# Two kinds of rows: operand pairs and plain rows that begin 32 bytes behind a multiple of 2048, beside rows that begin on one

## The chip, the core and the metric

The kernel runs on one core of a Trainium2 chip. The metric is the device time of one execution in microseconds (us); a smaller number is better. All times below come from runs of this kernel and from one execution that the hardware profiler recorded.

## The reference

Two layers of a block with four parallel branches work on a sequence of 512 tokens (the "x stream") and on a context of 256 tokens (the "context stream"), with a width of 1024. Per layer and stream:

```python
hx = modulate(rmsnorm(x, norm_w[l]), shift_x, scale_x)      # the same for the context
px = split_proj(hx @ w_in[l])                               # 1024 -> 11008 columns
r = head_group_norm(retention(px)) * silu(ret_z)            # branch 0
s = sc_b * conv3(sc_c * sc_x) * silu(sc_z)                  # branch 1
f = silu(layer_norm(conv31(a * sigmoid(g)))) * silu(cf_z)   # branch 2
a = windowed_gqa(px, context keys and values) * silu(att_z) # branch 3
merged = sum(sigmoid(gate_i) * (branch_i @ w_branch[i]))
x = x + gate_x * (merged @ w_out[l])
```

The context stream is computed in full in the first layer; in the second one only its keys and values are needed. The result is rmsnorm(x) * final_norm_w. Everything is float32.

## The kernel before

**Work.** Activations lie with the 1024 features on the 128 partitions, in 8 chunks, and with the tokens along the row. A product of full accuracy is made from three products of a fast format (fp32r): each operand is split into a high part (`hi`, made by ScalarE, ACT) and a low part (`lo`, what is left, made by VectorE, DVE), and TensorE (PE) adds hi·hi, hi·lo and lo·hi over the chunks:

```python
for j, (a, b) in enumerate(((hi, xh), (hi, xl), (lo, xh))):
    nc.tensor.matmul(ps, a[:, cs(i)], b.r[:, o:o + t], ...)
```

Here `a` is the weight block (stationary, 128 columns) and `b` the activation row (moving, `t` columns): 512 columns in the x stream, 256 in the context stream. These are the products with the outputs `d` in the profile. Each of them loads its own weights. Transposes and small products in plain float32 write the outputs `k` and `ov`.

**Stages in order of time.** Start (modulation vectors from the weights `w_m`, norm of the context, first projections): to about 50 us. Context stream of layer 0: to about 392 us. x stream of layer 0: to about 1090 us. Keys and values of the context in layer 1: to about 1120 us. x stream of layer 1 and the final norm: to the end.

**Rows.** Activations, split parts and many loaded weights live in 59 rows of 2048 bytes for each partition (128 x 512 float32 or fp32r) and 12 half rows. `Arena.get` hands out the row at the head of one list of free rows; a row comes back to the tail of the list when the Python object dies, which is when the last instruction that uses it has been recorded. What is handed out next to the same row has to wait on the chip until the last reader of the old content is done. `row()` gives a plain row, `part()` a row for one split part, and `pair()` for 256 columns gives one row for both parts (`r51h` in the first 1024 bytes, `r51l` behind it). A tile `fill` of 480 float32 stands ahead of the rows; in the built program it puts the first row at byte 18432 of a partition, which is 9 times 2048, so every row begins on a multiple of 2048 and every low half of a pair 1024 bytes behind one. The split weights `wh`, `wl` begin on multiples of 2048 as well.

**Order.** PE runs in the order in which the code issues its work. The other engines and the DMA queue of SyncE (SP), through which all loads go, run in an order that a scheduler chooses from the dependences, those through reused rows among them. In the start, `start()` loads per step four rows of `w_m` (`mod_load`), splits them (`mod_pe`) and multiplies them; in the first three steps it also splits a weight block that was loaded in two rows (`w_load`, `w_split`, output `wl`). The context stream loads its weights into rows too, the x stream mostly into two tiles of their own.

Of the kernel before, what the change touches and what calls it, by code (L numbers as in the profile page):

```python
# [8 lines left out]
F32 = mybir.dt.float32  # L9
# [16 lines left out]
P = 128  # L26
# [90 lines left out]
    return c  # L117


NROWS = 59  # L120
PAD = 480


class Row:
# [3 lines left out]
    def __init__(self, free, ring, tile, w, parts):  # L128
        self.free, self.ring = free, ring
        self.r = tile[:, :w] if parts else None  # L130
        self.a = tile[:, :w].bitcast(F32) if parts else tile[:, :w]
# [20 lines left out]
        self.ring = None  # L152


class Arena:


    def __init__(self, pool, n, nh):
        self.full = [pool.ring(2048, name=f"row{i}") for i in range(n)]
        self.half = [pool.ring(1024, name=f"hrow{i}") for i in range(nh)]  # L160
        self.n = 0

    def get(self, w, parts, keep, pair=False):
        free = self.half if keep and w <= 256 else self.full
        if not free:
            self.relief(free)
        ring = free.pop(0)
        self.n += 1
        if pair:
            both = Both(free, ring)  # L170
            return [Half(both, ring.tile([P, 256], F32R, name=f"r{self.n}{x}"), w, True) for x in "hl"]
        t = ring.tile([P, 256 if free is self.half else 512], F32R if parts else F32, name=f"r{self.n}")
        return Row(free, ring, t, w, parts)
# [104 lines left out]
class Block:  # L278
    def __init__(self, ctx, tc, xc, vec, cst, w_a, w_g, w_b, w_o, w_m, out):
        self.tc, self.nc = tc, Tally(tc.nc)  # L280
        self.xc, self.out = xc, out
        self.wsrc = {"a": w_a, "g": w_g, "b": w_b, "o": w_o}
        self.w_m = w_m

        rp = ctx.enter_context(tc.tile_pool(name="rp", bufs=1))
        rp.tile([P, PAD], F32, name="fill")
        self.arena = Arena(rp, NROWS, 12)
        self.arena.relief = self.relief

        self.cp = cp = ctx.enter_context(tc.tile_pool(name="cp", bufs=1))  # L290
        self.wraw = [cp.tile([P, 1024], F32, name=f"w{i}") for i in range(2)]
        self.wt = [[cp.tile([P, 1024], F32R, name=f"w{p}{i}") for p in "hl"] for i in range(3)]
        self.pt = [cp.tile([P, 640], F32, name=f"p{i}") for i in range(6)]
        pp = ctx.enter_context(tc.tile_pool(name="pp", bufs=1, space=PSUM))
        nc = self.nc
        self.cst = cp.tile([P, NC_], F32, name="cst")
        self.vec = cp.tile([P, NV], F32, name="vec")
        nc.sync.dma_start(self.vec, vec)
        nc.sync.dma_start(self.cst[:, :NCE], cst[:, :NCE])
        self.late_consts = lambda: nc.sync.dma_start(self.cst[:, NCE:], cst[:, NCE:])  # L300
        self.rings = {}
        self.dense = [pp.tile([P, 512], F32, name=f"d{i}") for i in range(3)]
        self.ovs = [pp.tile([P, 512], F32, name="ov")]
        self.work = [pp.tile([P, 512], F32, name=f"k{i}") for i in range(4)]
        self.turn = {}
        self.wq, self.wraws, self.wready, self.wkeep = [], [], {}, {}
        self.lanes = [[] for _ in range(5)]
        self.turns = 0
        self.flow = None
# [1161 lines left out]
```

## Time and profile before

| | |
|---|---|
| median of 3 runs | 1832.25 us (1831.04 to 1833.5) |
| the profiled execution | 1832.62 us, of which its span is 1830.5 us |
| PE busy | 1799.5 us, 98% of the span |
| weight loads (PEld) busy | 1562.1 us, 85% |
| DVE busy | 1329.4 us, 73% |
| ACT busy | 847.1 us, 46% |
| mean granted TensorE clock | 0.994 |

A matmul's busy time in the profile covers its way through the array, so that of neighbouring products overlaps (283 ns for one with 256 columns); what counts is the distance from the start of one to the start of the next, called spacing below. It is read from a row with starts, or as a count of products in a stretch.

### The profile page before, as it was taken

What the parts mean: (1) busy time and instruction counts of PE and PEld (TensorE: products, weight loads), DVE (VectorE), ACT (ScalarE), POOL (GpSimd) and SP (SyncE); (2) the same over time, 40 slices, a digit from 0 to 9 for tenths busy, and PEclk for the clock granted to TensorE, in tenths of its full rate; (3) what the DMA queues carried; (4) which work ended last, traced back from release to release, by engine and by line L of the source; (5) the groups of instructions that cost most, each with busy time, mean ns of one, the idle gap of its engine ahead of it and who ended that gap; (6) DMA issues with size and microseconds to landing.
All of it is one profiled execution on the core that took longest, in us unless ns stands there. A gap on an engine that the chain in (4) does not pass through costs nothing. (4 is left out here: it accounts for less than half of the span.)

```text
span 1830.5 us, 27546 instructions
## 1 busy us (share of the span) xinstructions
PE 1799.5 (98%) x10224; PEld 1562.1 (85%) x10224; DVE 1329.4 (73%) x2643; ACT 847.1 (46%) x1616; POOL 27.9 (2%) x34
## 2 busy tenths in 40 slices
PE   6999999999999999999999999999999999999997
PEld 4999999998888888788888889888888888888887
DVE  8899999884556669996898457447999865444445
ACT  6666765553554544423423336445534554323232
POOL 1000000000000000000000000000000000000000
PEclk8999999999999999999999999999999999999999
DMA  8736377743122222233555552322122222332233
GB/s 306 252 125 213 111 242 231 235 138 116 69 70 67 84 81 83 91 108 124 185 170 168 169 182 75 116 70 70 66 91 87 80 98 87 115 104 87 87 117 114
DMA packets 104646, 232.60 MB, mean 127 GB/s; under 512 B 12864, under 2 KB 20800, under 8 KB 104512
## 3 DMA queue, kind: packets, MB, share of 16 engines
q1 hardware_dynamic: 104512, 230.84, 37.9%
q8 instruction: 80, 1.31, 0.3%
q14 instruction: 54, 0.44, 0.1%
HBM read 218.73 MB, written 5.24 MB: 122 GB/s over the span
## 5 line engine op out<-in xcount | busy, mean ns | idle before, releaser
L187 PE MATMUL d<-r,wh 128*128 128x512 f32 (+1 forms) x3136 | 942.7, 383 | 0.3 <-DVE r L187 0.3
L187 PEld LDWEIGHTS d<-r,wh 128*128 128x128 f32 x3136 | 572.7, 188 | 106.2 <-DVE r L187 0.5
L187 PE MATMUL d<-r,wl 128*128 128x512 f32 (+1 forms) x1568 | 597.6, 381 | 0.0
L187 DVE TENSOR_TENSOR wl<-w,wh 128x1024 fp32r<-128x1024 f32 x193 | 235.6, 1221 | 233.8 <-ACT wh L187 229.0
L187 ACT ACTIVATE wh<-w 128x1024 fp32r<-128x1024 f32 x193 | 205.0, 1062 | 411.5 <-PE d L187 358.2
L187 PEld LDWEIGHTS d<-r,wl 128*128 128x128 f32 x1568 | 294.8, 188 | 57.6
L187 ACT ACTIVATE r<-r 128x512 fp32r<-128x512 f32 (+3 forms) x264 | 150.5, 588 | 211.6 <-DVE r L187 94.5
L187 DVE TENSOR_TENSOR r<-r,r 128x512 fp32r<-128x512 f32 (+5 forms) x338 | 207.8, 629 | 35.2 <-ACT r L187 31.2
L187 DVE SCALAR_TENSOR_TENSOR r<-r,h_cfw,r 128x503 f32<-128x503 f32 (+19 forms) x360 | 229.1, 648 | 2.0
L187 PE MATMUL d<-r,r 128*128 128x512 f32 x768 | 184.8, 389 | 0.5 <-DVE r L187 0.5
L187 ACT ACTIVATE wh<-r 128x512 fp32r<-128x512 f32 x208 | 129.2, 631 | 101.7 <-PE d L187 88.5
L187 PEld LDWEIGHTS d<-r,r 128*128 128x128 f32 x768 | 144.1, 188 | 30.8 <-DVE r L187 0.9
L187 DVE TENSOR_TENSOR wl<-r,wh 128x512 fp32r<-128x512 f32 x208 | 140.6, 685 | 18.6 <-ACT wh L187 17.5
L187 DVE SCALAR_TENSOR_TENSOR r<-r,d 128x512 f32<-128x512 f32 (+1 forms) x156 | 92.7, 594 | 56.4 <-PE d L187 32.4
L187 ACT ACTIVATE r<-d 128x512 f32<-128x512 f32 (+2 forms) x234 | 118.5, 507 | 14.1 <-PE d L187 9.5
L187 PE MATMUL k<-r,r 128*128 128x128 f32 (+2 forms) x752 | 112.3, 290 | 2.7 <-ACT p L187 2.6
L187 ACT ACTIVATE r<-k 128x512 fp32r<-128x512 f32 (+4 forms) x162 | 76.9, 522 | 70.5 <-PE k L187 69.2
L187 PEld LDWEIGHTS k<-r,r 128*128 128x128 f32 x752 | 99.5, 191 | 8.9 <-ACT p L187 6.2
L187 ACT ACTIVATE p<-k,s_nm 128x256 f32<-128x256 f32 (+1 forms) x144 | 69.7, 497 | 78.0 <-DVE s_nm L187 77.9
L187 DVE SCALAR_TENSOR_TENSOR r<-r,cs,r 128x256 f32<-128x256 f32 x196 | 83.6, 477 | 2.0 <-DMA r<-w_m 1.4
L187 DVE TENSOR_TENSOR r<-k,r 128x512 fp32r<-128x512 f32 (+2 forms) x88 | 54.4, 651 | 9.5 <-ACT r L187 9.3
L187 ACT ACTIVATE p<-p,s_rc 128x512 f32<-128x512 f32 (+2 forms) x80 | 51.3, 719 | 9.6 <-DVE s_rc L187 9.6
(393 smaller groups left out, 2245.3 us busy)
## 6 DMA issues: line engine op xcount, KB each, us to landing
w<-w_a SPq DMA_DIRECT2D x108, 512.0 KB, 3.5
r<-w_a SPq DMA_DIRECT2D x128, 256.0 KB, 5.0
w<-w_g SPq DMA_DIRECT2D x64, 512.0 KB, 3.5
r<-w_m SPq DMA_DIRECT2D x96, 256.0 KB, 3.8
r<-w_b SPq DMA_DIRECT2D x96, 256.0 KB, 3.4
r<-w_g SPq DMA_DIRECT2D x64, 256.0 KB, 3.8
w<-w_o SPq DMA_DIRECT2D x21, 512.0 KB, 3.5
r<-xc SPq DMA_DIRECT2D x24, 256.0 KB, 3.8
```

Source lines behind the costliest of these rows:

```text
L187: return f(*a, **k)
```

## The change

The rows now come in two lists. `full` holds 36 rows, which begin on multiples of 2048 as before; `odd` holds 24 rows in a pool of their own, behind a tile of 32 bytes, so they begin 32 bytes behind a multiple of 2048. A further tile of 504 float32 brings what follows (the split weights among it) back to a multiple of 2048. `Arena.get` looks through the lists in an order that depends on the use: a row for one split part of more than 256 columns comes from `full` if it has a free row, otherwise from `odd`; a plain row, and a pair for 256 columns, comes from `odd` if it has a free row, otherwise from `full`. In all there are 60 rows in place of 59.

```diff
-NROWS = 59
+NROWS = 36
+NODD = 24
 PAD = 480
@@
+class Kinds:
+    def __init__(self, lists):
+        self.lists = lists
+
+    def __bool__(self):
+        return any(self.lists)
+
+    def first(self):
+        return next(x for x in self.lists if x)
@@
-    def __init__(self, pool, n, nh):
+    def __init__(self, pool, n, odd, nodd, nh):
         self.full = [pool.ring(2048, name=f"row{i}") for i in range(n)]
         self.half = [pool.ring(1024, name=f"hrow{i}") for i in range(nh)]
+        self.odd = [odd.ring(2048, name=f"orow{i}") for i in range(nodd)]
@@
     def get(self, w, parts, keep, pair=False):
-        free = self.half if keep and w <= 256 else self.full
-        if not free:
-            self.relief(free)
+        if keep and w <= 256:
+            kinds = Kinds([self.half])
+        elif parts and not pair:
+            kinds = Kinds([self.full, self.odd])
+        else:
+            kinds = Kinds([self.odd, self.full])
+        if not kinds:
+            self.relief(kinds)
+        free = kinds.first()
         ring = free.pop(0)
@@
         rp = ctx.enter_context(tc.tile_pool(name="rp", bufs=1))
         rp.tile([P, PAD], F32, name="fill")
-        self.arena = Arena(rp, NROWS, 12)
+        ro = ctx.enter_context(tc.tile_pool(name="ro", bufs=1))
+        ro.tile([P, 8], F32, name="fill1")
+        self.arena = Arena(rp, NROWS, ro, NODD, 12)
+        rf = ctx.enter_context(tc.tile_pool(name="rf", bufs=1))
+        rf.tile([P, 504], F32, name="fill2")
```

In the built programs, 2688 of the 3488 products with 256 moving columns and 128 weight columns have their moving row 32 bytes behind a multiple of 64 after the change (of the 5248 with 512 columns, 136); before, it is none of either.

PE issues the same products in the same order up to about 850 us; from there on some transposes of the convolution branch stand a few products later. The other queues change from the start on. On SP in the start, before (`r52` to `r55` and `r68` to `r71` are rows of `w_m` for two steps, `r56` and `r57` the two halves of a weight block; in brackets the semaphores that the load waits for, DVE and PE for readers of the row's old content, DMAHW for earlier loads):

```order
L187 DMA r52_349<-w_m 128x512 [waits DMAHW2_49]
L187 DMA r53_350<-w_m 128x512 [waits DMAHW3_49]
L187 DMA r54_351<-w_m 128x512 [waits DMAHW4_49]
L187 DMA r55_352<-w_m 128x512 [waits DMAHW5_49]
L187 DMA r56_357<-w_a 128x512 [waits DMAHW6_49]
L187 DMA r57_358<-w_a 128x512 [waits DMAHW7_49]
L187 DMA r68_410<-w_m 128x512 [waits DMAHW0_49,DVE_49]
L187 DMA r69_411<-w_m 128x512 [waits DMAHW1_49,PE_49]
L187 DMA r70_412<-w_m 128x512 [waits DMAHW2_49,PE_49]
L187 DMA r71_413<-w_m 128x512 [waits DMAHW3_49,PE_49]
```

The same loads after the change:

```order
L210 DMA r52_358<-w_m 128x512
L210 DMA r53_359<-w_m 128x512 [waits DMAHW3_49]
L210 DMA r56_366<-w_a 128x512 [waits DMAHW4_49]
L210 DMA r57_367<-w_a 128x512 [waits DMAHW5_49]
L210 DMA r54_360<-w_m 128x512 [waits DMAHW6_49,DMAHW0_49,DVE_49]
L210 DMA r55_361<-w_m 128x512 [waits DMAHW7_49,DMAHW1_49,DVE_49]
L210 DMA r68_419<-w_m 128x512 [waits PE_49]
L210 DMA r69_420<-w_m 128x512 [waits DVE_49]
L210 DMA r70_421<-w_m 128x512 [waits DMAHW4_49,DMAHW2_49,DVE_49]
L210 DMA r71_422<-w_m 128x512 [waits DMAHW5_49,DMAHW3_49,DVE_49]
```

`r54` and `r55` now wait for DVE and stand behind `r56` and `r57`: they lie where `r39` and `r40` (the halves of the third weight block) lay, and `r70` and `r71` where `r56` and `r57` lie. Later in the start, `r110` lies where `r94` lay. On DVE at the same step, before (`wl2` is the low half of a weight block, a `TENSOR_TENSOR` with two rows the low part of a row of `w_m`):

```order
L187 TENSOR_TENSOR r75_427<-r53_350,r74_426 128x512
L187 SCALAR_TENSOR_TENSOR r66_404<-r6_183,mod0_164,r49_338 128x256
L187 TENSOR_TENSOR r77_435<-r54_351,r76_434 128x512
L187 TENSOR_TENSOR r79_443<-r55_352,r78_442 128x512
L187 TENSOR_TENSOR wl2_142<-r56_357,wh2_141 128x512
L187 TENSOR_TENSOR wl2_142<-r57_358,wh2_141 128x512
```

And after the change:

```order
L210 TENSOR_TENSOR r75_436<-r53_359,r74_435 128x512
L210 TENSOR_TENSOR wl2_151<-r56_366,wh2_150 128x512
L210 TENSOR_TENSOR wl2_151<-r57_367,wh2_150 128x512
L210 SCALAR_TENSOR_TENSOR r66_413<-r6_192,mod0_173,r49_347 128x256
L210 TENSOR_TENSOR r77_444<-r54_360,r76_443 128x512
L210 TENSOR_TENSOR r79_452<-r55_361,r78_451 128x512
```

The split of the weight block moved ahead of that of `r54` and `r55`.

## Rows read from the trace of the kernel before

**Rows 1.** The page's part 1: busy us (share) x instructions

```profile
PE 1799.5 (98%) x10224; PEld 1562.1 (85%) x10224; DVE 1329.4 (73%) x2643; ACT 847.1 (46%) x1616; POOL 27.9 (2%) x34
```

**Rows 2.** The page's part 2: tenths busy in 40 slices of 46 us

```profile
PE   6999999999999999999999999999999999999997
...
DVE  8899999884556669996898457447999865444445
...
PEclk8999999999999999999999999999999999999999
```

**Rows 3.** PE's waits in the whole span: us in total, times, longest

```profile
PE k L187 <- DVE r L187: 8.0, 6, 2.2
PE k L187 <- DVE s L187: 7.0, 1, 7.0
PE k L187 <- ACT p L187: 4.2, 12, 0.7
```

**Rows 4.** Busy time by windows, the start and the context stream: PE, PEld, DVE, ACT, POOL

```profile
0.00:52.00 52.00, 37.05 (x229) 25.14 (x229) 42.58 (x142) 33.66 (x70) 4.85 (x7) 0.87 0.91 318
...
60.00:368.00 308.00, 308.00 (x2572) 307.25 (x2571) 284.71 (x680) 188.34 (x416) 6.37 (x7) 1.00 0.60 196
```

**Rows 5.** Windows in the context stream, products with 256 columns alone

```profile
255.00:285.00 30.00, 30.00 (x252) 30.00 (x252) 28.02 (x64) 17.77 (x37) 0.00 (x0) 1.00 0.83 263
...
270.00:282.00 12.00, 12.00 (x102) 12.00 (x102) 10.50 (x23) 7.31 (x16) 0.00 (x0) 1.00 0.77 235
```

**Rows 6.** Windows in the x stream, products with 512 columns alone

```profile
1600.00:1768.00 168.00, 168.00 (x743) 139.12 (x742) 73.45 (x93) 49.41 (x70) 0.00 (x0) 1.00 0.29 99
1600.00:1612.00 12.00, 12.00 (x55) 9.93 (x54) 5.37 (x7) 3.44 (x5) 0.00 (x0) 1.00 0.24 88
```

**Rows 7.** PE's timeline behind an attention product, context stream: start, us, instruction

```profile
232.49 0.28 PE L187 MATMUL d<-r51l,wh 128*128 128x256 f32 x1
...
233.43 0.28 PE L187 MATMUL d<-r95h,wh 128*128 128x256 f32 x1
```

**Rows 8.** PE's timeline behind small float32 products, x stream

```profile
904.93 0.40 PE L187 MATMUL d<-r,wl 128*128 128x512 f32 x1
905.17 0.62 PE L187 MATMUL d<-r,wh 128*128 128x512 f32 x2
...
907.01 0.39 PE L187 MATMUL d<-r,wl 128*128 128x512 f32 x1
```

**Rows 9.** PE's timeline, plain float32 products and transposes with 128 columns

```profile
100.83 0.28 PE L187 MATMUL k<-r,r 128*128 128x128 f32 x1
100.94 0.60 PE L187 MATMUL k<-cst,r 128*128 128x128 f32 x4
```

**Rows 10.** The page's part 6, one row: count, KB each, median us to landing

```profile
r<-w_m SPq DMA_DIRECT2D x96, 256.0 KB, 3.8
```

**Rows 11.** SP's timeline in the start, loads merged

```profile
14.38 0.95 SPq L187 DMA_DIRECT2D r<-w_a  x2
15.63 2.28 SPq L187 DMA_DIRECT2D r<-w_m  x4
18.21 1.21 SPq L187 DMA_DIRECT2D r<-w_a  x2
20.51 14.93 SPq L187 DMA_DIRECT2D r<-w_m  x16
```

**Rows 12.** DVE's timeline in the start, last readers of reused rows

```profile
24.11 1.29 DVE L187 TENSOR_TENSOR wl<-r,wh 128x512 fp32r<-128x512 f32 x2
...
30.62 1.29 DVE L187 TENSOR_TENSOR wl<-r,wh 128x512 fp32r<-128x512 f32 x2
...
39.71 0.48 DVE L187 SCALAR_TENSOR_TENSOR r95l<-r,mod,r95h 128x256 fp32r<-128x256 f32 x1
```

**Rows 13.** ACT's timeline in the start, first readers of the later loads

```profile
26.87 1.65 ACT L187 ACTIVATE r<-r 128x512 fp32r<-128x512 f32 x3
...
31.43 2.17 ACT L187 ACTIVATE r<-r 128x512 fp32r<-128x512 f32 x4
...
39.96 1.66 ACT L187 ACTIVATE r<-r 128x512 fp32r<-128x512 f32 x3
```

## Prediction

> **What bounds the kernel now.** I read the page's parts 1 and 2 first. PE is busy for 1799.5 of 1830.5 us, while DVE has a quarter of the span free [rows 1]; in the slices PE shows 9 everywhere but in the first and the last one, at the full clock from the second slice on, and DVE shows 8 and 9 in the first quarter, the context stream, and half of that later [rows 2]. PE's waits are some 20 us in all [rows 3], nearly all in the first 52 us, where PE is busy for 37.05 us; from 60 to 368 us it has no idle time at all, while DVE works for 284.71 of these 308 us [rows 4]. So after the start the time is the number of products times their spacing, and there are two ways to change it: another spacing, or PE starting later into its closed stream. Whatever the start loses is not won back, because behind it PE has no gap in which to catch up.
>
> Busy PE is not PE at its peak, so I read the spacing next. In the context stream two windows that hold nothing but products with 256 columns differ by 150 products and 18 us, which makes 120.0 ns for each [rows 5]. In the x stream 688 products with 512 columns take 156 us, 226.7 ns each [rows 6]. [...]
>
> These two are the settled values. Behind an interruption by float32 products the spacing is another one for some products: in the context stream eight spacings, from `r51l` with `wh` at 232.49 us over the products of `r67` and `r81` to `r95h` at 233.43 us, take 0.94 us, 117.5 ns each [rows 7]; in the x stream nine spacings from 904.93 to 907.01 us take 2.08 us, 231.1 ns each [rows 8]. The same operands at the same places thus run 2.5 ns closer together (256 columns) or 4.4 ns further apart (512 columns) than when they have settled. So there is something in the reading of operands with which the stream falls into step, and the step that it settles in is the better one for 512 columns and the worse one for 256.
>
> **The change part by part.** *Moving rows of the context 32 bytes further.* This touches 2688 products, all with 256 columns, and 136 with 512. In the trace of before no moving row of this format begins anywhere but on a multiple of 512 bytes, so its price has no row. [...] Above, a product that loses its step as those with 512 columns do, 4.4 ns more: 2688 x 4.4 = 11.8 us more. I take the row for the same shape and operands out of step, 117.5 ns [rows 7]: 2688 x 2.5 = 6.7 us less. The reason for this value: a moving row that is shifted by eight elements against its weights, which stay where they were, should not settle in the same step. The reason against a larger gain: rows 7 are the shortest spacing that I found for this shape. The 136 products with 512 columns cost at most 136 x 4.4 = 0.6 us; I leave them out.
>
> [...]
>
> *Plain rows 32 bytes further.* They are operands of DVE and ACT and of the float32 products. On DVE and ACT a few ns would lie under PE's stream. The float32 products and transposes are about a tenth of the 10224 [rows 1]; a change of 1 ns there is 1 us, with no sign known, so nothing enters the sum.
>
> *Reuse of rows.* Before, a freed row went to the tail of one list of 59 and came back late. Now a plain row is taken from `odd` as long as that has a free one, so a row that was just freed is taken again while rows of `full` that were never used lie idle. More loads wait for DVE, and SP is one queue in order: all loads behind a waiting one wait too. In the start I price the loads that the order shows. `r54` and `r55` lie where `r39` and `r40` lay. Their last reader is the pair on DVE that starts at 24.11 us; with 0.69 us each they end at 24.80 and 25.40 [rows 12]. Before, the loads were issued at some 17.0 and 17.6 us, the third and fourth of four [rows 11]. With 3.8 us to landing [rows 10] they now land at 28.6 and 29.2 us, and ACT read them as second and third of three from 26.87 us, at 27.39 and 27.91 [rows 13]: 1.2 and 1.3 us late. `r70` and `r71` lie where `r56` and `r57` lay, read on DVE until 31.31 and 31.91 [rows 12]; they land at 35.1 and 35.7, and ACT read them as third and fourth of four from 31.43, at 32.47 and 32.99: 2.6 and 2.7 us late. `r110` waits until 40.19 for the reader of `r94` [rows 12], lands at 44.0 and was read at about 40.48: 3.5 us late. Bounds: nothing, if the order in which the loads and splits now stand hides it (DVE takes the weight block ahead of `r54`), and 1.3 + 2.7 + 3.5 = 7.5 us if each lateness is paid in full. I take 2.7 us, that of `r70` and `r71`: PE is still idle there between steps, while at 40 us DVE has other work to do in place of `r110`.
>
> Behind the start, the weight rows of the context are reused just as soon, but `w_ahead` keeps two blocks split and two more loaded in front of PE, and PE waits for nothing there [rows 4]; I put this at nothing. Its cover is DVE's free time, 308 - 284.7 = 23.3 us [rows 4]: if DVE, itself in order, stands still behind late loads for longer than that, PE pays the rest.
>
> *Sum.* -6.7 + 2.7 = -4.0 us. The profiled execution took 1832.62 us, 0.37 above the median; 1832.25 - 4.0 gives **1828.3 us**.
>
> **The rivals.** *The place of a row means nothing to PE.* For it speaks that high and low halves, 1024 bytes apart, run at the same spacing [rows 5]; against it that the spacing does depend on a step [rows 7, 8]. The spacing stays 120.0, only the start is left: 1832.25 + 2.7 = 1835.0, between 1832.3 and 1839.8. [...] The trace, where the same operands take two spacings [rows 7, 8], shows only that something beyond the columns counts, not that it is the memory.
>
> [...]
>
> *Late loads eat it up (slower).* Place: SP and DVE in the start and the context stream. Price: 7.5 us in the start, 1839.8 without a gain. It decides as soon as the lateness passes the gain of 6.7 us. For it: DVE is the engine on which most freed rows wait and has 7% free time in the context. Against: PE did not wait for weights once from 60 to 368 us.
>
> *The shifted step is a worse one (slower).* +11.8 + 2.7 gives 1846.8. For it: out of step the products with 512 columns take 4.4 ns more. Against: those with 256 take less.
>
> **How the numbers follow.** A measurement of this kernel can tell some 0.2%, 3.7 us, from no change. Forecast (spacing 116.5 to 119, start 0 to 4): chance 0.42, 1823 to 1834; 0.25 of it beyond 0.2%, 0.17 within. No effect of the place: 0.22, of it 0.13 within and 0.09 slower. A good part of the extra cycles: 0.14, faster. Late loads: 0.14, of it 0.11 slower, 0.02 within and 0.01 faster. Worse step: 0.08, slower. Together faster 0.40, within 0.32, slower 0.28. The range of 1815 to 1842 leaves out the lower half of the third case, the worse step and the tail of the late loads, some 2 in 10; the forecast's own range is 1823 to 1834.
>
> **What would show each step right or wrong.** Spacing: the count of products in the windows from 255 to 285 us (a smaller spacing gives more than 252), and the distances of single starts in the timeline; 226.7 must stay in the x stream. Start: PE's busy time in the first 52 us below 37 us, and waits of SP for DVE there. Reuse: idle time of PE between 60 and 368 us, where there is none now, released by DVE `wl`. Wrong would be a spacing of 120.0 or above, a start that is later by more than 5 us, or a difference that lies in the x stream.

## The result, and the profile after

The changed kernel takes 1860.36 us (median of 4 runs, 1859.19 to 1862.79) beside 1831.64 us for the kernel before on the same chip: slower, ratio 1.0159, 95% interval 1.0147 to 1.0172. Forecast were 1828.3 us and a range up to 1842; the rival that late loads eat the gain up was on the right side, at 1839.8, but forecast 7.5 us more where 28.7 were measured. The profiled execution took 1859.19 us, its span 1857.2.

The page's part 1, and of part 2 PE, DVE and PE's clock:

```profile
PE 1808.3 (97%) x10224; PEld 1565.4 (84%) x10224; DVE 1330.2 (72%) x2643; ACT 844.5 (45%) x1616; POOL 27.3 (1%) x34
...
PE   6999999989999999999999999999999999999997
...
DVE  7899989875447669995898467447989856343445
...
PEclk9999999999999999999999999999999999999999
```

Beside [rows 1, 2] nearly nothing shows: the same instructions, PE busy for 8.8 us more, one 8 in the ninth slice (371 to 418 us). The windows say more. Busy time by windows (PE, PEld, DVE, ACT, POOL, clock, DMA share, GB/s):

```profile
0.00:52.00 52.00, 36.97 (x212) 24.98 (x213) 40.28 (x131) 32.55 (x66) 4.84 (x7) 0.93 0.81 260
...
60.00:368.00 308.00, 301.00 (x2519) 298.36 (x2517) 279.67 (x665) 182.63 (x412) 5.02 (x6) 0.99 0.61 191
255.00:285.00 30.00, 29.21 (x248) 29.01 (x247) 21.99 (x48) 18.13 (x40) 0.00 (x0) 1.00 0.73 231
1600.00:1768.00 168.00, 168.00 (x743) 139.07 (x742) 72.76 (x96) 51.96 (x75) 0.00 (x0) 1.00 0.33 104
```

From 60 to 368 us PE stands idle for 7.0 us, where it had no gap [rows 4], and DVE works 5.0 us less in the same time than before. The x stream has its 743 products as before [rows 6]. PE's waits in the whole span (us, times, longest):

```profile
PE k L210 <- DVE r L210: 11.0, 8, 2.4
PE k L210 <- ACT p L210: 8.5, 10, 2.7
...
PE d L210 <- ACT wh L210: 5.4, 2, 3.8
...
PE d L210 <- ACT r L210: 2.5, 5, 0.8
```

Beside [rows 3] the waits of the outputs `d` for split weights (`wh`, and `r` for those of `w_b`) are new but for 0.2 us: PE comes to products whose weights aren't there.

**Where the 26.7 us of the two spans went.** PE's 10224 matmuls are the same in both, in the same order but for some transposes. So I took the starts of four of them (numbers 228, 3048, 6424 and 6668, counted from 0) and of the last (10223) from each trace; the distances are the lengths of the stages. All kernels of this study by that measure, in us (before was run again beside each group of kernels, and each ratio is to the runs on the same chip; the stages of a row come from its one profiled execution, which in e4 is the fastest of four, 2.7 us below the median):

| kernel | median | ratio to before (95%) | start | context, layer 0 | x, layer 0 | context, layer 1 | x, layer 1 |
|---|---|---|---|---|---|---|---|
| before | 1830.93 to 1831.64 | | 51.9 | 340.7 | 697.3 | 30.1 | 703.4 |
| after | 1860.36 | 1.0147–1.0172 | 54.5 | 354.8 | 701.0 | 29.5 | 710.3 |
| e1 aligned | 1858.36 | 1.0136–1.0164 | 53.3 | 357.6 | 698.0 | 30.1 | 710.1 |
| e2 place alone | 1847.61 | 1.0076–1.0104 | 53.0 | 337.0 | 706.3 | 29.8 | 713.3 |
| e3 all by age | 1829.58 | 0.9986–1.0003 | 50.5 | 334.3 | 700.6 | 29.5 | 704.3 |
| e4 loads by age | 1840.21 | 1.0040–1.0071 | 50.7 | 337.1 | 700.4 | 29.5 | 710.5 |
| e5 others by age | 1842.13 | 1.0040–1.0068 | 52.0 | 346.2 | 701.7 | 29.6 | 704.2 |
| e6 all shifted | 1832.87 (one run) | | 52.0 | 340.7 | 697.6 | 30.1 | 703.3 |
| e8 by age, 20 | 1829.77 | 0.9982–1.0000 | 50.7 | 335.6 | 699.6 | 29.4 | 703.7 |
| e9 stride alone | 1848.59 (one run) | | 52.1 | 337.5 | 707.2 | 29.9 | 713.0 |
| e10 weights 32 | 1828.28 | 0.9970–0.9988 | 52.9 | 337.4 | 696.5 | 29.8 | 702.7 |
| e11 weights 64 | 1824.72 | 0.9945–0.9972 | 53.2 | 335.0 | 697.2 | 29.6 | 700.9 |
| e12 weights 256 | 1831.33 | 0.9990–1.0009 | 50.3 | 340.7 | 696.6 | 30.1 | 703.2 |
| e13 weights 128 | 1828.00 | 0.9970–0.9988 | 51.0 | 338.8 | 696.5 | 30.0 | 703.2 |

The change costs 2.6 us in the start, 14.1 in the context stream, 3.7 and 6.9 in the x streams, and gains 0.6 in the second context stage. In the context stream the distances of successive starts can be sorted further. Distances within 16 ns of the settled 120.0 and 226.7 are spacing: they sum to 6.1 us less than before. Distances with over 0.4 us of idle time sum to 13.5 us more. Those in between, mostly products at the lower clock (0.50 to 0.52, below) behind such a wait, sum to 6.6 us more: -6.1 + 13.5 + 6.6 = 14.0.

**What late means here.** At 281 us, PE's timeline (start, us, instruction, idle time before and its releaser):

```profile
280.92 0.28 PE L210 MATMUL d<-r135l,wh 128*128 128x256 f32 x1
281.03 0.28 PE L210 MATMUL d<-r135h,wl 128*128 128x256 f32 x1
282.10 0.38 PE L210 MATMUL d<-r440h,r 128*128 128x256 f32 x1 [0.79 <-ACT r L210]
```

PE waits for a split of `w_b`. Where such a split comes from is seen in the timelines of DVE, SP and ACT in the microseconds ahead of it:

```profile
274.34 0.69 DVE L210 TENSOR_TENSOR r<-r,r 128x512 fp32r<-128x512 f32 x1 [1.34 <-ACT r L210]
274.95 0.68 DVE L210 TENSOR_TENSOR wl<-r,wh 128x512 fp32r<-128x512 f32 x1
275.55 0.68 DVE L210 TENSOR_TENSOR r<-r,r 128x512 fp32r<-128x512 f32 x1
...
279.99 0.69 DVE L210 TENSOR_TENSOR r<-r,r 128x512 fp32r<-128x512 f32 x1 [2.36 <-ACT r L210]
```

```profile
275.06 0.33 SPq L210 DMA_DIRECT2D r<-w_b  x1
275.66 0.33 SPq L210 DMA_DIRECT2D r<-w_g  x1
276.26 0.33 SPq L210 DMA_DIRECT2D r<-w_b  x1
...
280.71 0.33 SPq L210 DMA_DIRECT2D r<-w_b  x1
```

```profile
269.65 0.63 ACT L210 ACTIVATE r<-r 128x512 fp32r<-128x512 f32 x1 [4.57 <-DMA r<-w_b]
...
273.68 0.63 ACT L210 ACTIVATE r<-r 128x512 fp32r<-128x512 f32 x1 [2.09 <-DMA r<-w_b]
...
279.33 0.63 ACT L210 ACTIVATE r<-r 128x512 fp32r<-128x512 f32 x1 [3.19 <-DMA r<-w_b]
```

Each load leaves 0.03 us behind the end of an instruction of DVE (274.34 + 0.69 = 275.03, then 275.06; 275.63, 275.66; 276.23, 276.26; 280.68, 280.71): the row into which it writes is the one that DVE has just read (in the built program the first and the last of the four write at byte 143392, where DVE read until 275.03 and until 280.68). ACT, idle since 276.14, can begin on the first of these loads at 279.33, 4.3 us from its issue; DVE stands idle for ACT, and only behind its next instruction does the next row come free. Load, ACT, DVE and the row go round in a closed ring. This turn takes 5.65 us (273.68 to 279.33 on ACT), of which the 4.3 through DMA are the most; the turn before it took 4.03 (from 269.65). ACT's waits for loads, 52 to 410 us, after and (second fence) before:

```profile
ACT wh L210 <- DMA r<-w_g: 24.8, 11, 5.9
ACT r L210 <- DMA r<-w_b: 22.7, 15, 4.6
...
ACT wh L210 <- DMA r<-w_a: 19.1, 17, 2.7
```

```profile
ACT r L187 <- DMA r<-w_b: 3.9, 5, 1.7
```

Loads waited for readers on DVE before the change too: SP's waits for DVE `r` and `wl` from 52 to 410 us were 73.5 + 71.5 = 145.0 us, and are 88.5 + 104.6 = 193.1 now. What is new is that ACT then waits for the loads.

The longest wait in the context stream, 3.8 us at 389 us, is of the same kind. A load of `w_o` leaves at 389.06, 0.03 us behind the end of the instruction on DVE that read its row; ACT waits for it, and PE for ACT (SP, ACT, PE). Before, the last eight loads of `w_o` left in one group (second fence):

```profile
389.06 0.33 SPq L210 DMA_DIRECT2D r<-w_o  x1
...
392.17 0.63 ACT L210 ACTIVATE wh<-r 128x512 fp32r<-128x512 f32 x1 [1.30 <-DMA r<-w_o]
...
392.85 0.58 PE L210 MATMUL d<-r580h,wh 128*128 128x256 f32 x1 [3.78 <-ACT wh L210]
```

```profile
365.42 7.81 SPq L187 DMA_DIRECT2D r<-w_o  x8
```

**What a wait costs besides.** At 132 us a transpose waits for DVE. I take it that DVE had its weight splits late and its other work behind them; no run shows that by itself:

```profile
132.05 0.28 PE L210 MATMUL d<-r133h,wh 128*128 128x256 f32 x1
...
132.64 0.28 PE L210 MATMUL d<-r135h,wl 128*128 128x256 f32 x1
135.30 0.44 PE L210 MATMUL k<-cst,r 128*128 128x128 f32 x2 [2.38 <-DVE r L210]
...
137.87 0.69 PE L210 MATMUL k<-cst,r 128*128 128x128 f32 x2 [1.52 <-DVE wl L210]
...
138.57 0.41 PE L210 MATMUL d<-r51l,wh 128*128 128x256 f32 x1
138.78 0.41 PE L210 MATMUL d<-r51h,wl 128*128 128x256 f32 x1
139.00 0.41 PE L210 MATMUL d<-r67h,wh 128*128 128x256 f32 x1
...
142.84 0.31 PE L210 MATMUL d<-r135h,wh 128*128 128x256 f32 x1
```

```profile
132.00:135.00 3.00, 0.92 (x8) 0.71 (x7) 2.93 (x8) 1.71 (x5) 0.00 (x0) 1.00 0.65 184
...
138.00:140.50 2.50, 2.50 (x13) 2.50 (x14) 2.44 (x8) 2.50 (x10) 0.00 (x0) 0.50 0.34 105
```

Ahead of the wait five spacings from 132.05 to 132.64 take 118 ns each. Behind it and a second wait of 1.5 us the granted clock is 0.50 (138 to 140.5 us), and products are some 213 ns apart; 20 such spacings in a row, from 138.57 to 142.84 us, are 20 x (213 - 118) = 1.9 us on top of the waits. The same follows the wait of 3.8 us at 389 us, with 23 spacings (from 393.96 to 398.87 us) at a granted clock of 0.50 and 0.52 (393 to 396 and 396 to 399 us). Behind a wait of 1.6 us at 401.6 us it does not: the granted clock stays at 1.00 (401.5 to 405 us).

### The profile page after: what moved, and what is told of

The parts are those of the page before. It is cut to its first block, busy times and chain, and to the rows that moved or that the text cites. A ratio compares the mean times of both kernels' runs of the same rounds, so it can differ in the third digit from the quotient of the medians.

```text
span 1857.2 us, 27528 instructions
## 1 busy us (share of the span) xinstructions
PE 1808.3 (97%) x10224; PEld 1565.4 (84%) x10224; DVE 1330.2 (72%) x2643; ACT 844.5 (45%) x1616; POOL 27.3 (1%) x34
## 4 chain that ended last, share of the span: by engine, by line
PE 49%; issue 2%; ACT 1%; DVE 1%; POOLq 0%; POOL 0%; DVEq 0%; ACTq 0%
PE d L210 43%; PE k L210 5%; PE ov L210 1%; ACT p L210 1%; DVE r L210 1%; ACT wh L210 0%; DVE wl L210 0%; DVE s_mc L210 0%; POOLq L1492 0%; POOL s_rs L210 0%; DVEq L1492 0%; ACT r L210 0%; DVE s_mx L210 0%; DVE s_es L210 0%; DVE s_rc L210 0%
## 5 line engine op out<-in xcount | busy, mean ns | idle before, releaser
L210 DVE SCALAR_TENSOR_TENSOR r<-r,h_cfw,r 128x503 f32<-128x503 f32 (+14 forms) x360 | 231.8, 650 | 2.5
L210 PE MATMUL k<-cst,r 128*128 128x128 f32 (+1 forms) x372 | 50.2, 262 | 6.3 <-DVE r L210 4.8
```

The lines of the kernel that those rows point to most:

```text
L210: return f(*a, **k)
```

## The experiments

Theory A: rows are retaken too soon, so loads are late; the place itself only gains. Its rivals: B, the 32 bytes cost loads or engines something; C, it isn't the loads' rows but the other plain rows (ACT and DVE writing where another engine still reads).

**e1, the order of use without the place.** `fill1` is left out, and `fill2` made up:

```diff
-        ro.tile([P, 8], F32, name="fill1")
-        rf.tile([P, 504], F32, name="fill2")
+        rf.tile([P, 512], F32, name="fill2")
```

> The two lists and their order of use as after the change, but both kinds of rows begin on multiples of 2048 (the 32 bytes are taken out). Theory A, rows are retaken too soon: a freed plain row is taken again at once, its load has to wait on SP for the last reader on DVE, and the weights come late; the place is only good for PE. Then the loss stays and the gain of some 7 us goes: 1860 to 1868 us. PE should show the waits of 1 to 4 us at the same products of the context stream (numbers 887, 2083, 2953) and a spacing of 120.0 ns. Theory B, the 32 bytes cost the loads or the engines something: the loss goes with them, 1831 to 1836 us.

Measured: 1858.36 us. B falls: with all rows on multiples of 2048 the loss is there, at the same products (behind numbers 887, 2953 and 3001 in the context stream, 8021 and 8377 in the x stream; the long wait behind 2083 is not there). That it is a little below my 1860 is a result by itself: in the context stream the place is worth only 2.8 us here (357.6 to 354.8), though its spacing gains 6.1. The rest of the gain PE waits away: distances with a long wait are some 4 us more in the change than in e1. That the ring of the loads doesn't turn faster when PE does would explain it; this is not tested.

**e3, all plain rows by age.** The two lists stay, with the place. A list notes when each row was freed, and a plain row is taken from the list whose first row was freed earlier:

```diff
+    def append(self, ring):
+        Aged.n += 1
+        Aged.at[id(ring)] = Aged.n
+        list.append(self, ring)
...
     def first(self):
+        if self.aged:
+            return min((x for x in self.lists if x), key=lambda x: Aged.at.get(id(x[0]), 0))
         return next(x for x in self.lists if x)
...
-            kinds = Kinds([self.odd, self.full])
+            kinds = Kinds([self.odd, self.full], not pair)
```

> As after the change, with 36 rows on multiples of 2048 and 24 rows 32 bytes behind, but a plain row is taken from the list whose first row has been free for longer (pairs from odd first, split parts from full first, as in the change). Theory A: the loss goes and the gain stays: 1831.6 - 7.5 plus about 194 products of 512 columns at some 8 ns more (1.6 us) = 1826 us, 1823 to 1830. Theory B: plain rows are loaded and read 32 bytes behind as often as in the change, so 1850 us or more. Theory C, it isn't the loads but other users of retaken rows (ACT and DVE writing into rows that PE or the other engine still reads): the same as A here.

Measured: 1829.58 us, 31 us below the change. The context stream takes 334.3 us, 6.4 less than before. PE's waits there, 52 to 410 us, are

```profile
PE d L222 <- DVE wl L222: 0.7, 1, 0.7
PE d L222 <- ACT r L222: 0.2, 1, 0.2
```

But the x stream of layer 0 keeps 3.3 us of loss: in both x streams together 286 products of 512 columns have an operand 32 bytes behind (their spacing is 232 to 235 ns), and a wait of 1.2 us for `mod_flow` at 859 us stays. So gain and loss cancel, and it can't be told from before.

**e4 and e5, the two sorts of plain rows apart.** In e4 only rows that a load writes are taken by age, in e5 all others (the first added line is e4's, the second e5's; the calls that take a row for a load say so with `load=True`, not shown):

```diff
-            kinds = Kinds([self.odd, self.full])
+            kinds = Kinds([self.odd, self.full], load)
+            kinds = Kinds([self.odd, self.full], not pair and not load)
```

> As after the change, but only the rows that a load writes (weights, w_m, x) are taken by age from the two lists; all other plain rows come from odd first as in the change. Theory A, late loads on SP: nearly as in the run with all plain rows by age, 1825 to 1833 us. Theory C, other users of retaken rows: the loss stays for the most part, 1845 to 1860 us.

> The complement of the run with the loads by age: the rows that a load writes are taken from odd first as in the change, all other plain rows by age from the two lists. From the two runs, the loads account for some 20 us of the 31 between the changed kernel (1860.4) and the one with all by age (1829.6), the other rows for 10.6. Theory A (loads are the larger part, and the two add up): 1860.4 - 10.6 = 1850, between 1843 and 1856. Theory C (the other rows are what holds the chain up, and the loads gain only because they leave odd rows to them): below 1840.

Measured: 1840.21 and 1842.13. Neither A nor C alone: both sorts cost, in different stages. Both lie between the two theories' forecasts. In the context stream the loads' rows alone cost 346.2 - 334.3 = 11.9 us (e5 against e3), the others' alone 2.8 (e4 against e3), both together 20.5 (the change against e3), more than the sum. By the starts of single products the 20.5 lie in three places: 6.6 at 132 to 144 us of the changed kernel (of the loads' rows alone nothing, of the others' alone 2.4), 5.7 at 281 to 347 us, where the ring above turns (6.0 and 0.5), and 8.4 at 383 to 409 us, with the late loads of `w_o` (4.2 and nothing); the rest is -0.2. So the ring of `w_b` is a quarter of the loss there, and at 132 us both sorts are needed for the most of it. In e5 ACT waits for `w_b`, from 52 to 410 us,

```profile
ACT r L222 <- DMA r<-w_b: 44.6, 21, 4.7
```

In the x stream of layer 1, where most weights are loaded into tiles of their own, it is the other way round: 710.5 in e4 and 704.2 in e5, so the 6 us there come from the other rows alone. The waits that go with them are for `p` on ACT, the longest 2.7 us, at 1398 and 1475 us of the changed kernel; which row starts that chain stays open. No run separates the waits for rows on the chip from the other order that the scheduler chose for the queues; all that is shown is that both go with the order in which rows are retaken.

**e8, 40 rows and 20** in place of 36 and 24, by age.

> By age as before, with 40 rows on multiples of 2048 and 20 rows 32 bytes behind in place of 36 and 24. Pairs 32 bytes behind: 2808 products of 256 columns in place of 2976 (168 x 2.6 ns = 0.4 us more); split parts of 512 columns with an operand 32 bytes behind: 106 in place of 286 (180 x 6.5 ns = 1.2 us less). Theory A: 1829 us, 1826 to 1831, so faster than before by some 2 us if anything. If rows run short in another place, it shows as new waits of PE and the time is above 1831.

Measured: 1829.77, interval up to no change. The x stream of layer 0 gets 1.0 us back and the context stream loses 1.3.

**e2, e6 and e9, the place alone.** All three use the one list of 59 rows, so nothing is retaken sooner. e2: rows 2112 bytes apart, pairs 32 bytes behind the row's start; e9: the same without the 32 bytes; e6: `PAD = 488`, which moves rows and weights alike.

```diff
-        self.full = [pool.ring(2048, name=f"row{i}") for i in range(n)]
+        self.full = [pool.ring(2112, name=f"row{i}") for i in range(n)]
...
+            return [Half(both, ring.tile([P, 256 + o], F32R, name=f"r{self.n}{x}")[:, o:], w, True)
+                    for x, o in (("h", 8), ("l", 0))]
```

> One list of 59 rows in the order of before; rows 2112 bytes apart, and within a row the two halves of a pair begin 32 and 1056 bytes behind its start, all other tiles on its start (so a moving row of 512 columns on a multiple of 64). No row is retaken sooner than before. Theory A: only the gain is left; 2880 products at the 2.6 ns that the changed kernel gained for each are 7.5 us, so 1824 us (1823 to 1826), if a multiple of 64 is enough for the 226.7 ns of 512 columns. If these need a multiple of 2048, the half of them that lies on odd multiples of 64 would cost up to 2100 x 8 ns = 17 us and the time be up to 1841. Theory B says 1831 or more here, if what costs is the pair's place; if it is the place of the loaded rows, it can't be told from A.

> The kernel before with its first tile 32 bytes longer: every row and every split weight block, moving and stationary operands alike, begins 32 bytes behind a multiple of 2048. Theory D, what counts is how the operands of successive products lie to each other: spacings stay 120.0 and 226.7 ns, 1829 to 1833 us. Theory E, what counts is the place of the moving row itself: 117 ns for 256 and some 234 ns for 512 columns, 3488 x -2.8 + 5248 x 7 = +27, so 1858 us.

> Rows 2112 bytes apart in one list of 59 as in the run with the place alone, but without the 32 bytes in the pairs: high halves on the row's start, low halves 1024 bytes behind, all on multiples of 64. Theory D (the step is kept only while all operands lie on one grid of 2048): some 118 and 231.5 ns as with the 32 bytes, 1847 us. Theory F (it was the 32 bytes that broke the step of the 512 columns too): 120.0 and 226.7 ns, 1831 us.

Measured: 1847.61, 1832.87 and 1848.59. Windows of e9 and of e6 (products with 256 and with 512 columns):

```profile
255.00:285.00 30.00, 30.00 (x255) 30.00 (x255) 28.22 (x63) 16.47 (x34) 0.00 (x0) 1.00 0.83 272
1600.00:1768.00 168.00, 168.00 (x725) 135.98 (x724) 71.38 (x90) 48.78 (x69) 0.00 (x0) 1.00 0.29 94
```

```profile
255.00:285.00 30.00, 30.00 (x252) 30.00 (x252) 28.01 (x63) 17.65 (x37) 0.00 (x0) 1.00 0.82 264
1600.00:1768.00 168.00, 168.00 (x742) 139.10 (x742) 73.82 (x94) 49.44 (x70) 0.00 (x0) 1.00 0.30 99
```

e6 is the kernel before, 252 products [rows 5] and 742 beside 743 [rows 6], though every moving row lies 32 bytes behind. So theory D holds: what counts is how the moving row and its weights lie to each other. In e9 the rows lie at any multiple of 64 against weights on multiples of 2048, with no 32 bytes anywhere, and both spacings change: 255 and 725 products, the mean distance being some 118 ns for 256 and 231.7 ns (168 / 725) for 512 columns. My estimate for e2 had assumed that a multiple of 64 does for 512 columns, or at worst that half of them suffer, for 17 us; e2's x streams take 18.9 us more than before (706.3 + 713.3 beside 697.3 + 703.4).

**e10 to e13, the weights of the context moved instead of the rows.** One list of 59 rows on multiples of 2048, as before. The split weight blocks lie in wider tiles, six half rows fill the places between them, and a block for products of 256 columns begins `o` elements behind (the cut shows `o` for 32 bytes):

```diff
-        parts = [self.take("wt")]
+        o = 8 if key[3] or key[:2] == ("o", DEPTH - 1) else 0
+        parts = [[x[:, o:o + 1024] for x in self.take("wt")]]
```

> The one list of 59 rows of before, all on multiples of 2048 and retaken as before; instead, the split weight blocks wh, wl of the context's products (and of the last 256-column products at the end) begin 32 bytes behind a multiple of 2048, in the same tiles whose first byte the x stream's blocks use. 2880 products of 256 columns have their weights shifted against their rows, none of 512. Theory D (only how the operands lie to each other counts, and the loss of the change came from retaken rows alone): 2880 products at some 117.2 in place of 119.8 ns give 7.5 us, no new waits: 1823.5 us, 1822 to 1826. Theory G (it has to be the moving row that is shifted): 1831.

> The same with 64 bytes in place of 32. Theory D with any shift doing as well: some 117 to 118 ns, 1823 to 1826. If whole 64 bytes are one place for PE: 120.0 and 1831.

> The same with 256 bytes. If only the place within 64 or 128 bytes counts, it is as without a shift, 120.0 ns and 1831; if any shift against a grid of 512 bytes and more breaks the step, 117 to 118 ns and 1823 to 1826.

> As the runs with the context's weight blocks 32, 64 and 256 bytes behind, with 128 bytes. 32 gave 118.3 ns and 1828.3 us, 64 gave 116.2 ns and 1824.7 us, 256 gave 119.9 ns and 1831.3 us (unchanged). If the place within 256 bytes counts, 128 bytes is as good as 64 or better: 116 ns or less, 1822 to 1825. If only the place within 128 bytes counts: 120 ns and 1831.

Measured: 1828.28 with 32 bytes, 1824.72 with 64, 1828.00 with 128, 1831.33 with 256. The mean distances of the shifted products in closed stretches (products of one width that follow each other without an interruption) are 118.3, 116.2, 118.8 and 119.9 ns. 256 bytes are as none. D holds for e10 to the kind: moving the weights does what moving the rows does, with less gain than I gave it (337.4 against 340.7 us in the context stream). My guess that 128 would do as well as 64 was wrong. The windows from 60 to 368 us of e11 and e12, beside 2572 products in [rows 4]:

```profile
60.00:368.00 308.00, 307.72 (x2611) 305.40 (x2610) 288.28 (x691) 190.00 (x422) 6.38 (x7) 1.00 0.62 199
```

```profile
60.00:368.00 308.00, 308.00 (x2566) 306.78 (x2565) 284.09 (x676) 188.04 (x415) 6.38 (x7) 1.00 0.61 197
```

e11 is the best version found: ratio 0.9958, interval 0.9945 to 0.9972. It has the gain of the place in both context stages and in the last products, and pays nothing in the x streams.

## Why the prediction was wrong

**Spacing: right, in what it hangs on and in size.** Forecast were 6.7 us for 2688 products, from a spacing of 117.5 out of step. The trace gives 6.1 us less in the context stream and, sorted in the same way, 0.6 in the second context stage and 0.2 at the end: 6.9. That a moving row shifted by eight elements against its weights "should not settle in the same step" is what e6 and e10 show: with rows and weights shifted alike 252 products start in 30 us, as before, and with the weights alone shifted the mean distance is 118.3 ns. What the step is that the prediction reads out of [rows 7, 8] no run shows.

To its third case, a good part of the extra cycles, the prediction gave 0.14. No run shows how much of the 120.0 ns is extra; 32 bytes gave means of 117.2 ns (the change) and 118.3 (e10), and the closer of two stretches of e11, shown in the last section, has 113.1. That the place of a row means nothing to PE is refuted for this kernel as far as spacing goes: 64 bytes change it most of the four shifts of the weights, to a mean of 116.2 ns (e11) beside 120.0 before.

**The start: its steps are seen, its price is not settled.** `r54` leaves behind the reader of `r39`, at 24.69 us in SP's timeline of the changed kernel, where the prediction had 24.80. The stage is 2.6 us longer, beside the 2.7 forecast. But the same stage takes from 50.3 to 53.2 us in seven kernels that use the rows of the start in the order of before (e2, e6, e9 to e13), and 51.9 before. One execution each can't tell 2.6 us from that.

**Reuse behind the start: the step that failed.** The prediction says "I put this at nothing", with DVE's free time, 23.3 us, as the cover. Measured: 20.5 us in the context stream (the change against e3) and some 6 in the x stream of layer 1. The error lies in the sort of cover. I compared busy time with free time, as if DVE's idle time could be spent where it was needed. The delay isn't work, though, but the length of a ring: load, ACT, DVE, free row, load. Before, a row lay idle for a round of 59, so the next loads were under way while the last ones were being split, and the 4 us of a load (in the median 3.4 us for `w_b` and 3.8 for `w_g`, part 6 of the page of before) cost PE no wait from 60 to 368 us [rows 4]. With the row handed back at once, the load for the next block leaves only when DVE is done with the last one, and such turns (4.0 and 5.65 us above) make the weights late from 281 to 347 us; the late loads of `w_o` at 389 us come about in the same way. DVE meanwhile has more free time than before (308 - 279.7 = 28.3 us), not less. For the 6.6 us at 132 us and the 6 in the x stream of layer 1 only the order of reuse is shown to be the cause, not the steps in between. "`w_ahead` keeps two blocks split and two more loaded" was true in the order of the code; the two "more loaded" were late on the chip.

**The rival of late loads** had the place right, SP and DVE in the start and the context, but took its price, 7.5 us, from the start alone. What it lacked is the waits behind the start (13.5 us in the context stream), that they are paid again at the lower clock (0.50 to 0.52, most of 6.6 us there), and that the x stream of layer 1, with 27% of DVE's time free in the whole [rows 1], suffers as well.

**The x stream of layer 0** was left out of the sum, its 136 products at "at most 136 x 4.4 = 0.6 us". It lost 3.7 us, and a difference in the x stream was one of the prediction's own signs of being wrong. The 136 were those with a shifted moving row; in the built program 62 more have their weights, which lie in rows there, 32 bytes behind. In e1, without the place, it is 0.7; so most is the place there, in products of 512 columns (232 to 235 ns in place of 227, not 231.1) and in waits that go with it.

**One reading** was off without a term that hangs on it: PE's idle time is not nearly all in the first 52 us. Of 31.0 us, 15.0 lie there and 9.3 in the last 59 us (PE busy for 49.72 us from 1771 to 1830).

## What to carry to other kernels

A free list is part of the schedule: whoever hands out again a row that has just come back makes the next load wait for the last reader, and turns a prefetch into a ring of which the latency of a load is the most (4.3 of 5.65 us here). Price such a change by the ring (last reader, issue, landing, first reader) beside the time in which PE uses up one block, not by the free time of an engine. And when an operand's place is to be changed, change it where nothing else hangs on it: here the weights of one kind of product, not the rows that all share.

## What the runs showed of the hardware

- In this kernel the spacing of products that load weights each time hangs on how the moving row lies to its weights, not on either place alone: with both 32 bytes further it stays as before (e6, 252 products in 30 us and 742 in 168). For 256 columns: 120.0 ns with no shift, means of 117.2 (rows 32 bytes behind, the changed kernel), 118.3, 116.2 and 118.8 (weights 32, 64, 128 bytes behind), 119.9 with 256. For 512 columns the unshifted 226.7 is the best that was seen; other places gave means of 231.7 (e9) and 233 (rows or weights 32 bytes behind, e3).
- With 64 bytes closed stretches show two spacings: in e11 13 spacings from 189.82 to 191.29 us take 113.1 ns each, and 14 from 174.73 to 176.38 take 117.9, with operands of the same kind:

```profile
174.73 0.28 PE L187 MATMUL d<-r133h,wh 128*128 128x256 f32 x1
...
176.38 0.28 PE L187 MATMUL d<-r81h,wl 128*128 128x256 f32 x1
...
189.82 0.28 PE L187 MATMUL d<-r51h,wl 128*128 128x256 f32 x1
...
191.29 0.28 PE L187 MATMUL d<-r123h,wh 128*128 128x256 f32 x1
```

  A third of e11's distances in closed stretches are 113 or 114. What decides which of the two it will be stays open, and so do the causes of both.
- Two waits of PE of 2.4 and 1.5 us, with six small products between them, were followed by 20 spacings of some 213 ns at a granted clock of 0.50, 1.9 us more; a wait of 3.8 us by 23, at 0.50 and 0.52. Behind one wait of 1.6 us the granted clock stayed at 1.00.
